# Attention of a hybrid block, written in a fixed order: two mixers' groups in turn, branch pieces in quarters

## The chip, the cores and the metric

The kernel runs on one core of one Trainium2 chip. The metric is the device time of one execution in microseconds (us), the median of a few runs. The core has five queues that work side by side: PE (TensorE, matmuls), DVE (VectorE), ACT (ScalarE), POOL (GpSimd) and SP, which issues all the DMAs here. Each takes its instructions in the order in which they stand in the program.

## The reference

One layer on x of 2048 rows and 1024 columns, all in float32. A projection feeds two attention mixers and their gates:

```python
xn = rms_norm(h, norm_gain[layer])
qa, ka, va, ga, qb, kb, vb, gb, iq, ik, iw, za, zb = jnp.split(xn @ w_in[layer], offsets, axis=-1)
ya = chunked_relpos_attention(qa, ka, va, rel_bias[layer]) * jax.nn.silu(ga)   # 8 heads, own chunk of 64 and 8 before
yb = dsa_sparse_attention(qb, kb, vb, iq, ik, iw) * jax.nn.silu(gb)            # 8 heads on one K and V, 256 keys a query
merged = sigmoid(za + b_merge[0]) * (ya @ w_branch_a) + sigmoid(zb + b_merge[1]) * (yb @ w_branch_b)
out = rms_norm(h + merged @ w_out, final_norm_gain)
```

In mixer B an indexer picks the 256 keys of each query; the kernel turns that choice into an additive mask and computes B as a dense attention over all keys up to the query's chunk.

## The kernel before

**Stages.** The first half projects x, searches the 256 keys and writes q, k, v, gates and masks to DRAM. From about 980 us on attention runs, overlapping the end of the projection; then the merged product with w_out and the last norm.

**Numbers in two halves.** A float32 operand is split into a high part (rounded by an ACT copy) and a low part (value less high part), and products take hi and lo matmuls.

**Units.** Mixer A has 32 units: a group G of 512 rows by one of 8 heads. Mixer B has 64: a block b of 128 rows by u, a pair of heads; its work grows with b, over b + 1 tiles of 128 keys. A unit's first half, one(), makes scores: for a segment of up to 512 keys two matmuls into one of two PSUM banks `s`, then one DVE instruction (L942) that adds bias or mask, writes P to SBUF and keeps the running extreme mx; when a row block is complete ACT takes the exp of it in place (L1021 for A, L1129 for B). The second half, two(), goes in packs of up to four 128x128 tiles: transposes of P into one of three PSUM banks `pt` (L1051, L1143), split() into `pth` (ACT) and `ptl`, then products with V into one of two banks `O` (L1061, L1151). A unit then closes: the halves of O are added (ACT, DVE), scaled by the sums and the gate, and split into the tiles ya or yb of its group.

**split().** With EVERY = 3 two packs of three have ACT write `pth` (L965) and DVE subtract (L966); the third has ACT write `pth` (L958) and a second copy `pf` (L959), and POOL subtract (L963), since POOL is given SBUF operands alone.

**Branch pieces.** When a group of 512 rows is complete in a mixer, branch(m, G, c) multiplies it with one of 8 column tiles of w_branch: loads dst and sig, ACT and POOL split the weight (L1189, L1190), 12 matmuls into bank `d` (helper mm3, L238), a DVE product with the gate (L1196) and a store, or, for the second mixer to reach a group, a load of the first's result, a POOL sum (L1203) and a store. There are 64 pieces; the 8 of mixer B's last group run in the tail.

**Order.** attention() takes the units in a list `seq`, A's group 0 first, then A and B mixed so that both keep pace by a cost table. It steps one() of the next unit and two() of this one in turn. Pieces come 2 (A) or 4 (B) after one unit, from a unit or two past their group. A scheduler that simulates the engines then reorders the instructions of each queue. DMAs of a unit stand two units ahead on SP.

Of the kernel before, what the change touches and what calls it, by code (L numbers as in the profile page):

```python
# [8 lines left out]
F32 = mybir.dt.float32  # L9
# [16 lines left out]
H = 8  # L26
# [7 lines left out]
EVERY, MODE = 3, 1  # L34
# [29 lines left out]
WARM = 22  # L64
WIDE = 0.8
# [32 lines left out]
def block_kernel(ctx: ExitStack, tc: tile.TileContext, io, dbg=None):  # L98
# [834 lines left out]
    def next_o(shape):  # L933
        i = rot("O", 2 if late else 1)
        return (pe, pl_ps)[i].tile(shape, F32, name="O", tag=f"O{i}")

# [8 lines left out]

    def split(hi, lo, src, n):
        turn[0] += 1
        if MODE == 3:
            c = n * SPL // 128
            nc.scalar.activation(hi, src, AF.Copy)  # L950
            pf = wk.tile([128, 512], F32, name="pf", tag="pf", bufs=PFB)[:, :n - c]
            nc.scalar.activation(pf, src[:, c:], AF.Copy)
            nc.vector.tensor_tensor(lo[:, :c], src[:, :c], f32(hi[:, :c]), op=OP.subtract)
            nc.gpsimd.tensor_tensor(lo[:, c:], pf, f32(hi[:, c:]), op=OP.subtract)
        elif EVERY and turn[0] % EVERY == 0:
            pf = wk.tile([128, 512], F32, name="pf", tag="pf", bufs=PFB)[:, :n]
            if MODE == 1:
                nc.scalar.activation(hi, src, AF.Copy)  # L958
                nc.scalar.activation(pf, src, AF.Copy)  # L959
            else:  # L960
                nc.scalar.activation(pf, src, AF.Copy)
                nc.gpsimd.tensor_copy(hi, pf)
            nc.gpsimd.tensor_tensor(lo, pf, f32(hi), op=OP.subtract)  # L963
        else:
            nc.scalar.activation(hi, src, AF.Copy)  # L965
            nc.vector.tensor_tensor(lo, src, f32(hi), op=OP.subtract)  # L966
# [3 lines left out]
    def load_a(G, h):  # L970
# [8 lines left out]
        v = ld.tile([128, 8, 128], F32R, name="vs", tag="vs")  # L979
        for i, g in enumerate(range(max(0, G - 1), G + 1)):  # L980
            nc.sync.dma_start(f32(kk[:, i * 512:i * 512 + 512]), kA[g].rearrange("l r h n -> (l r) h n")[:, h, :])
            nc.sync.dma_start(f32(v[:, 4 * i:4 * i + 4]), vA[g][h])
# [3 lines left out]
        return base, q, kk, v, bias  # L986

    def a_unit(G, h):
        st = {}

        def loads():
            st["ld"] = load_a(G, h)
            if h % 2 == 0:
                sg = ld.tile([128, 512], F32, name="sg", tag="sg", bufs=SGB)
                nc.sync.dma_start(sg, gAD[G][(h // 2) * 128:(h // 2) * 128 + 128])
                shared["sg", "a", h // 2] = sg

        def one():
            base, q, kk, v, bias = st["ld"]
            P = next_p()  # L1000
            P = P[:, :2560].rearrange("p (j n) -> p j n", j=4)
            st["P"] = P
            mx = shared["mx"] = sml.tile([128, 4], F32, name="mx", tag="mx", bufs=4)
            if h % 2 == 0:
                shared["sum", "a", h // 2] = sml.tile([128, 2, 4], F32, name="sum", tag="sum", bufs=4)
            sm = shared["sum", "a", h // 2]
            for j in range(4):
                i = 4 * G + j
                f = max(0, i - 4)
                nk = (i - f + 1) * 128  # L1010
                segs = [(0, 256), (256, 384)] if nk == 640 else [(0, nk)]
                for a, w in segs:
                    s_ps = next_s()
                    ko = (f - base) * 128 + a
                    for m in range(2):
                        nc.tensor.matmul(s_ps[:, :w], q[:, m, j * 128:(j + 1) * 128], kk[:, ko:ko + w],
                                         start=(m == 0), stop=(m == 1))
                    softmax_piece(s_ps[:, :w], bias[:, 640 - nk + a:640 - nk + a + w], a == 0,
                                  P[:, j, a:a + w], mx[:, j:j + 1])
                    yield  # L1020
                nc.scalar.activation(P[:, j, :nk], P[:, j, :nk], AF.Exp, bias=mx[:, j:j + 1], scale=-1.0,  # L1021
                                     accum_out=sm[:, h % 2, j:j + 1])

        def two():
            base, q, kk, v, bias = st["ld"]
            P = st["P"]
            O = next_o([128, 512])
# [5 lines left out]
            packs = []  # L1033
            while tiles:
                p_, room = [tiles.pop(0)], 4
                room -= p_[0][2]
                for z in list(tiles):
                    if z[2] <= room:
                        p_.append(z)
                        tiles.remove(z)  # L1040
                        room -= z[2]
                packs.append(p_)
            done = 0
            total = sum(len(p_) for p_ in packs)
            for p_ in packs:
                pt = next_pt([128, 512])
                off = 0
                for kt, j0, nj in p_:
                    for j in range(j0, j0 + nj):
                        f = max(0, 4 * G + j - 4)  # L1050
                        nc.tensor.transpose(pt[:, off:off + 128], P[:, j, (kt - f) * 128:(kt - f + 1) * 128], ident)  # L1051
                        off += 128
                ph_ = wk.tile([128, 512], F32R, name="pth", tag="pth", bufs=HB)
                pl_ = wk.tile([128, 512], F32R, name="ptl", tag="ptl", bufs=HB)
                split(ph_[:, :off], pl_[:, :off], pt[:, :off], off)
                yield
                off = 0
                for kt, j0, nj in p_:
                    w = nj * 128
                    for n_, src in enumerate((ph_, pl_)):  # L1060
                        nc.tensor.matmul(O[:, j0 * 128:j0 * 128 + w], v[:, kt - base, :], src[:, off:off + w],  # L1061
                                         start=(done == 0 and n_ == 0), stop=(done == total - 1 and n_ == 1),
                                         skip_group_check=True)
                    done += 1
                    off += w
            ty = wy.tile([128, 512], F32, name="ty", tag="ty", bufs=TYB)
            if h % 2 == 0:
                shared["y"] = wy.tile([128, 512], F32, name="y", tag="y")
            y = shared["y"]
            a0, a1 = (slice(0, 64), slice(64, 128)) if h % 2 == 0 else (slice(64, 128), slice(0, 64))  # L1070
            nc.scalar.activation(ty[a0], O[a1], AF.Copy)
            nc.vector.tensor_tensor(y[a0], O[a0], ty[a0], op=OP.add)
            yield
            if h % 2 == 1:
                yield from finish("a", G, h // 2, y, shared.pop(("sum", "a", h // 2)), shared.pop(("sg", "a", h // 2)),
                                  slice(0, 512))

        return loads, one, two

    shared = {}  # L1080

    def finish(m, G, pair, y, sm, sg, cols):

        n = 4
        nc.vector.reciprocal(sm, sm)
        rb = wz.tile([128, n, 2, HD], F32, name="rb", tag="rb", bufs=1)
        nc.gpsimd.tensor_copy(rb, sm.rearrange("p a j -> p j a")[:, :, :, None].to_broadcast([128, n, 2, HD]))
        rp = next_pt([128, 512])
        for j in range(n):
            nc.tensor.transpose(rp[:, j * 128:(j + 1) * 128], rb[:, j].rearrange("p a d -> p (a d)"), ident)  # L1090
        nc.vector.tensor_tensor(sg, rp, sg, op=OP.mult)
        nc.gpsimd.tensor_tensor(y, y, sg, op=OP.mult)
        yield
        yh, yl = y_of(m, G)
        nc.scalar.activation(yh[:, pair, cols], y, AF.Copy)
        nc.gpsimd.tensor_tensor(yl[:, pair, cols], y, f32(yh[:, pair, cols]), op=OP.subtract)

    def b_unit(b, u):

        n = 128 * (b + 1)  # L1100
        st = {}

        def loads():
            if u == 0:
                q = ldb.tile([128, H, 128], F32R, name="qsB", tag="qsB")
                nc.sync.dma_start(f32(q), qB[b // 4][b % 4].rearrange("l r h n -> (l r) h n"))
                sg = ldb.tile([128, 4, 128], F32, name="sgB", tag="sgB")
                nc.sync.dma_start(sg, gBD[b // 4].rearrange("(c p) n -> p c n", p=128)[:, :, (b % 4) * 128:(b % 4 + 1) * 128])
                if b < 2:
                    mk = mk01[:, b, :]  # L1110
                else:
                    mk = ldb.tile([128, S], BF16, name="mk", tag="mk")
                    nc.sync.dma_start(mk[:, :n], mskD[b, :, :n])
                shared["b", b] = (q, sg, mk)
# [17 lines left out]
        def two():  # L1132
            P = st["P"]
            if u % 2 == 0:
                shared["OB"] = next_o([128, 4, 128])
# [642 lines left out]
```

## Time and profile before

| | us |
|---|---|
| median of 3 runs | 2018.23 |
| the runs | 2017.92 to 2023.54 |
| profiled execution | 2020.23 |
| its span, first to last instruction | 2018.3 |

| engine | busy us | share of the span |
|---|---|---|
| PE | 1968.9 | 98% |
| DVE | 1442.0 | 71% |
| ACT | 1267.2 | 63% |
| POOL | 810.7 | 40% |

Matmuls are pipelined and their ends are modelled, so a PE that is busy 98% of the time is not one at its peak pace: waits of a tenth of a microsecond between two matmuls do not show as idle time. The distance between the starts of matmuls tells more. PEld is TensorE's weight load, which overlaps the matmuls. In the rows, "x" and a number is a count; names are out<-in.

### The profile page before, as it was taken

To read this page: it belongs to the slowest core of one execution; us is meant where nothing else is said; L and a number is where in the kernel's file an instruction comes from. 1 tells how busy PE (TensorE), PEld (TensorE's weight loads), DVE (VectorE), ACT (ScalarE), POOL (GpSimd) and SP (SyncE) were. 2 spreads that over 40 slices of the span, in tenths; PEclk is the share of its full clock that TensorE was granted. 3 is DMA by queue.
4 is the path that set the end of the run, shared out by engine and by line. 5 is a ranking of instruction groups with operands and counts; after the bars stand their busy time and mean duration, and the time that the engine had idled before them with its cause. 6 is when DMAs were issued, how large, how long until landed. Compare 5 with 4: busy or idle time off the path is not lost. (4 is left out here: it accounts for less than half of the span.)

```text
span 2018.3 us, 34087 instructions
## 1 busy us (share of the span) xinstructions
PE 1968.9 (98%) x10699; PEld 1689.3 (84%) x10699; DVE 1442.0 (71%) x3584; ACT 1267.2 (63%) x2540; POOL 810.7 (40%) x1057
## 2 busy tenths in 40 slices
PE   9999999999999999899989999999999999999998
PEld 8788888899898888678768888888988898887886
DVE  6638788797988988565556778658875688765444
ACT  6446666565476655354587879759986698773221
POOL 2222233322262454553345564464445444442420
PEclk9999999999999999999999999999999999999999
DMA  9673444555465665388998564573356531335732
GB/s 340 216 237 122 133 140 153 178 169 166 157 205 170 220 208 188 111 261 273 305 277 272 173 203 144 178 233 120 119 159 203 175 102 53 111 89 183 227 134 94
DMA packets 244731, 363.16 MB, mean 180 GB/s; under 512 B 31169, under 2 KB 115777, under 8 KB 244417
## 3 DMA queue, kind: packets, MB, share of 16 engines
q1 hardware_dynamic: 244544, 360.94, 55.8%
q8 instruction: 85, 1.39, 0.3%
q14 instruction: 102, 0.83, 0.1%
HBM read 244.23 MB, written 116.62 MB: 179 GB/s over the span
## 5 line engine op out<-in xcount | busy, mean ns | idle before, releaser
L238 PE MATMUL acc<-xh,wt 128*128 128x512 f32 x2128 | 675.5, 391 | 5.1 <-DVE wt L1393 1.6
L238 PEld LDWEIGHTS acc<-xh,wt 128*128 128x128 f32 x2128 | 398.5, 188 | 90.1 <-DVE wt L1393 2.7
L238 PE MATMUL acc<-xl,wt 128*128 128x512 f32 x1064 | 415.0, 390 | 0.1
L963 POOL TENSOR_TENSOR ptl<-pf,pth 128x512 fp32r<-128x512 f32 (+1 forms) x144 | 179.7, 1248 | 221.1 <-ACT pf L959 176.1
L238 PEld LDWEIGHTS acc<-xl,wt 128*128 128x128 f32 x1064 | 199.9, 188 | 40.8 <-DVE xl L1386 0.4
L966 DVE TENSOR_TENSOR ptl<-pt,pth 128x512 fp32r<-128x512 f32 (+1 forms) x288 | 187.0, 659 | 44.9 <-ACT pth L965 44.0
L617 DVE SCALAR_TENSOR_TENSOR sc<-lg,iw,sc 128x512 f32<-128x512 f32 (+2 forms) x266 | 178.1, 678 | 44.1 <-ACT lg L612 39.1
L1126 PE MATMUL s<-kBt,qsB 128*128 128x512 f32 (+3 forms) x640 | 188.9, 386 | 6.4 <-DMA kBt<-kB 3.2
L229 POOL TENSOR_TENSOR wt<-wst,wt 128x512 fp32r<-128x512 f32 (+1 forms) x96 | 115.9, 1236 | 182.1 <-ACT wt L228 165.6
L612 ACT ACTIVATE lg<-lg 128x512 f32<-128x512 f32 (+2 forms) x304 | 150.4, 524 | 49.5 <-PE lg L610 48.4
L965 ACT ACTIVATE pth<-pt 128x512 fp32r<-128x512 f32 (+1 forms) x288 | 159.6, 578 | 29.4 <-PE pt L1143 16.1
L1129 ACT ACTIVATE P<-P,mx 128x128 f32<-128x128 f32 (+15 forms) x128 | 154.6, 1209 | 23.0 <-DVE mx L942 22.1
L1143 PE MATMUL pt<-ident,P 128*128 128x128 f32 x1088 | 166.9, 274 | 1.8 <-DVE ptl L966 1.0
L1151 PE MATMUL O<-pth,vBt 128*128 128x256 f32 x544 | 148.4, 291 | 3.2 <-DVE yb L1161 1.1
L1151 PE MATMUL O<-ptl,vBt 128*128 128x256 f32 x544 | 148.0, 298 | 2.7 <-POOL ptl L963 1.3
L942 DVE CUSTOM_DVE_ANT_0 P<-s,mk,mx 128x512 f32<-128x512 f32 (+2 forms) x192 | 125.2, 652 | 28.7 <-PE s L1126 20.9
L1143 PEld LDWEIGHTS pt<-ident,P 128*128 128x128 f32 x1088 | 126.9, 140 | 10.8 <-DVE ptl L966 2.3
L1190 POOL TENSOR_TENSOR dw<-dst,dw 128x512 fp32r<-128x512 f32 x64 | 82.5, 1290 | 109.0 <-ACT dw L1189 108.2
L1126 PEld LDWEIGHTS s<-kBt,qsB 128*128 128x128 f32 x640 | 103.5, 192 | 19.6 <-DVE mx L942 10.0
L665 ACT ACTIVATE jk<-sc,st 128x640 int8<-128x640 f32 (+6 forms) x49 | 71.2, 1453 | 75.1 <-DVE st L683 63.5
L1151 PEld LDWEIGHTS O<-ptl,vBt 128*128 128x128 f32 x544 | 103.0, 189 | 12.8 <-DVE ptl L966 6.4
L1151 PEld LDWEIGHTS O<-pth,vBt 128*128 128x128 f32 x544 | 103.2, 190 | 11.0 <-ACT pth L965 3.4
(323 smaller groups left out, 4459.3 us busy)
## 6 DMA issues: line engine op xcount, KB each, us to landing
wst<-wP SPq DMA_DIRECT2D x80, 256.0 KB
wst<-wS SPq DMA_DIRECT2D x72, 256.0 KB
kk<-kA SPq DMA_DIRECT2D x56, 256.0 KB
vs<-vA SPq DMA_DIRECT2D x56, 256.0 KB
wst<-wS SPq DMA_DIRECT2D x72, 192.0 KB
qz<-qA SPq DMA_DIRECT2D x96, 128.0 KB
qD<-q SPq DMA_DIRECT2D x39, 256.0 KB
part<-qD SPq DMA_DIRECT2D x39, 256.0 KB
```

Source lines behind the costliest of these rows:

```text
L229: nc.gpsimd.tensor_tensor(wt[:, 1, k:k + n, c * 128:(c + 1) * 128], st, f32(hi), op=OP.subtract)
L238: m = nc.tensor.matmul(acc, a, b, start=(first and i == 0), stop=(last and i == n - 1), **({} if first and last else {"skip_group_check": ...
L612: nc.scalar.activation(lg, lg, AF.Relu)
L617: nc.vector.scalar_tensor_tensor(o_, lg, wv, o_, op0=OP.mult, op1=OP.add)
L942: nc.vector.tensor_tensor_reduce(dst, ps_, add, 1.0, FMAX if first else mx, OP.add, OP.min, accum_out=mx)
L963: nc.gpsimd.tensor_tensor(lo, pf, f32(hi), op=OP.subtract)
L965: nc.scalar.activation(hi, src, AF.Copy)
L966: nc.vector.tensor_tensor(lo, src, f32(hi), op=OP.subtract)
L1126: nc.tensor.matmul(s_ps[:, :w], q[:, h, :], kBt[:, m, a:a + w], start=(m == 0), stop=(m == 1))
L1129: nc.scalar.activation(P[:, e, :n], P[:, e, :n], AF.Exp, bias=mx[:, e:e + 1], scale=-1.0, accum_out=st["sum"][:, (u % 2) * 2 + e:(u % 2) * ...
L1143: nc.tensor.transpose(pt[:, k, e, :], P[:, e, (kt + k) * 128:(kt + k + 1) * 128], ident)
L1151: nc.tensor.matmul(o_, vBt[:, kt + k, :], src[:, k, :], start=(kt + k == 0 and n_ == 0), stop=(kt + k == b and n_ == 1), skip_group_check= ...
```

## The change

- EVERY goes from 3 to 6: one pack in six is split on POOL, not one in three.
- attention() now ends before unit 6 has been multiplied with V; the rest runs in written(), in which the order of all five queues is the order of the code, with no scheduler.
- `seq` takes whole groups in turn: A's 0, B's blocks 0 to 3 (one A unit among them), the rest of A's 1, B's 4 to 7, A's 2, B's 8 to 11, A's 3, B's 12 to 15.
- A unit is cut into score(n), turned(n) and closing(). written() counts events; an event is one segment of scores or one pack of transposes. Scores run ahead by 1.3 to 2.2 units. later(d, f) puts a step d events on: an exp 2, the low half 0, the product with V 6 or when three wait.
- A piece is an object: its loads, then 8 events on the weight's high half, then four parts of three matmuls. fill() hands out parts so that the pieces of a group end before the other mixer's next group is through.
- V, B's q with the mask, and the gates have loads of their own, at the place where their buffer comes free. The six one-column POOL copies ahead of the kBt and vBt loads are gone. Five weights of w_out and the first m tile come in steps during the last units and pieces.

The count of matmuls and of DMAs is the same. DVE has 72 subtractions more, ACT 72 copies and POOL 72 subtractions fewer.

```diff
-EVERY, MODE = 3, 1
+EVERY, MODE = 6, 1
...
-    seq = [("a", 0, h) for h in range(H)]
-    ua = [("a", g, h) for g in range(1, NG) for h in range(H)]
-    ub = [("b", b, u) for b in range(4 * NG) for u in range(4)]
...
+    seq = [("a", 0, h) for h in range(H)]
+    for i in range(4 * 4):
+        seq.append(("b", i // 4, i % 4))
+        if i in (6,):
+            seq.append(("a", 1, (6,).index(i)))
+    for g in range(1, NG):
+        seq += [("a", g, h) for h in range(H) if ("a", g, h) not in seq]
+        seq += [("b", b, u) for b in range(4 * g, 4 * g + 4) for u in range(4)]
...
+        while t_[0] < len(units):
...
+            if si < len(units) and si <= ti + 2 and ps - pt_ < 1 + min(LEADB if isinstance(units[si], BUnit) else LEADA, LEADE / events[si]):
+                exp = units[si].score(s_[1])
...
+                run_due()
+                if exp:
+                    later(EXPD, exp)
+            else:
+                if t_[1] == 0:
+                    unit_starts(ti)
+                while len(products) >= BEHIND:
+                    made[0] += 1
+                    multiply()
...
+                low, times_v = units[ti].turned(t_[1])
...
+                run_due()
+                later(LOWD, low)
+                later(OD, lambda n=n: due_product(n))
+            fill(min(t_[0], len(units) - 1), t_[1] / len(units[t_[0]].packs) if t_[0] < len(units) else 1)
+            background()
...
-    for _ in att_gen:
-        pass
-
-    load_m(0)
+    E_ = mybir.EngineType
+    with tc.manual_schedule(engines={E_.PE, E_.DVE, E_.Activation, E_.Pool, E_.SP}):
+        written()
```

The order on PE among large B units, before (s are scores, pt transposes of P, O products with V, hi from pth and lo from ptl):

```order
L1143 MATMUL pt<-ident,P 128x128 x4
L1126 MATMUL s<-kBt,qsB 128x512 x2
L1151 MATMUL O<-pth,vBt 128x256
L1126 MATMUL s<-kBt,qsB 128x512 x2
L1151 MATMUL O<-ptl,vBt 128x256
L1151 MATMUL O<-pth,vBt 128x256
L1151 MATMUL O<-ptl,vBt 128x256
L1143 MATMUL pt<-ident,P 128x128 x2
```

The same engine in mixer B after the change, with a quarter of a piece (d, from a group ya of mixer A and its weight dw):

```order
L1188 MATMUL pt<-ident,P 128x128 x4
L1175 MATMUL s<-kBt,qsB 128x512 x2
L1175 MATMUL s<-kBt,qsB 128x256 x2
L1201 MATMUL O<-pth,vBt 128x256
L1201 MATMUL O<-ptl,vBt 128x256
L1188 MATMUL pt<-ident,P 128x128 x4
L254 MATMUL d<-ya_16847,dw 128x512
L254 MATMUL d<-ya_16848,dw 128x512
L254 MATMUL d<-ya_16847,dw 128x512
L1175 MATMUL s<-kBt,qsB 128x512 x2
```

Before, the scheduler set scores between a high product and its low one; now a pack's products stand together, after the next packs' transposes. A piece before stands on PE like this, between scores of mixer A and transposes of mixer B:

```order
L1016 MATMUL s<-kk,qz 128x256 x2
L1143 MATMUL pt<-ident,P 128x128 x2
L238 MATMUL d<-yb_14570,dw 128x512
L238 MATMUL d<-yb_14571,dw 128x512
L238 MATMUL d<-yb_14570,dw 128x512 x2
L238 MATMUL d<-yb_14571,dw 128x512
L238 MATMUL d<-yb_14570,dw 128x512 x2
```

All twelve matmuls follow each other there; after the change no more than three do (the fence before). On ACT among large B units before, with the exp (P), the high halves and the second copies:

```order
L1129 ACTIVATE P,sumB<-P,mx 128x1792
L958 ACTIVATE pth<-pt 128x512
L959 ACTIVATE pf<-pt 128x512
L965 ACTIVATE pth<-pt 128x512 x2
L1129 ACTIVATE P,sumB<-P,mx 128x1792
L958 ACTIVATE pth<-pt 128x512
```

And on ACT after, with a piece's weight (dw):

```order
L1179 ACTIVATE P,sumB<-P,mx 128x1792
L993 ACTIVATE pth<-pt 128x512 x3
L1272 ACTIVATE dw<-dst 128x512
L1179 ACTIVATE P,sumB<-P,mx 128x1792
L993 ACTIVATE pth<-pt 128x512
L990 ACTIVATE pth<-pt 128x256
```

The exp keeps its place among the packs, three to four of them from one to the next; half of the second copies are gone.

More of the change, by code (lines that the diff above doesn't have):

```diff
@@ L64 @@
 WARM = 22
+AT8 = 5
+MSTEP = 2
+LASTA = 3
+ADD = 2
+READY = 5
+GAP = 4
+OD = 6
+PREP = 8
+MARGIN = 4
+LEADA = 0.3
+LEADB = 1.2
+LEADE = 5
+EXPD = 2
+LOWD = 0
+BEHIND = 3
+GATES = 6
 WIDE = 0.8
@@ L944, in block_kernel @@
     turn = [PH]
[L946 to L966, printed above, removed]
     qz = []
@@ L1010, in one @@
                 nk = (i - f + 1) * 128
[L1011 to L1027, printed above, removed]
+                for a, w in [(0, 256), (256, 384)] if nk == 640 else [(0, nk)]:
+                    self.segs.append((j, (f - base) * 128 + a, a, w, nk))
             tiles = []
@@ L1041, in two @@
                         room -= z[2]
[L1042 to L1046, printed above, removed]
-                off = 0
[L1048 to L1058, printed above, removed]
+                self.packs.append(p_)
@@ new lines, in turned, with times_v @@
+        def turned(self, n):
+            pt = next_pt([128, 512])
+            off = 0
+            for kt, j0, nj in self.packs[n]:
+                for j in range(j0, j0 + nj):
+                    f = max(0, 4 * self.G + j - 4)
+                    nc.tensor.transpose(pt[:, off:off + 128], self.P[:, j, (kt - f) * 128:(kt - f + 1) * 128], ident)
+                    off += 128
+            ph_ = wk.tile([128, 512], F32R, name="pth", tag="pth", bufs=HB)
+            pl_ = wk.tile([128, 512], F32R, name="ptl", tag="ptl", bufs=HB)
+            low = splitter(ph_[:, :off], pl_[:, :off], pt[:, :off], off)
+            def times_v():
+                if n == 0:
+                    self.O = bank_of([128, 512])
+                off = 0
+                for kt, j0, nj in self.packs[n]:
@@ L1063, in two @@
                                          skip_group_check=True)
-                    done += 1
+                    self.done += 1
                     off += w
[L1066 to L1096, printed above, removed]
@@ new lines, in branch @@
+    def branch(m, G, c):
+        p_ = Piece(m, G, c)
+        p_.fetch()
+        p_.high()
+        p_.low()
+        for k in range(4):
+            p_.part(k)
+        p_.out()
+        p_.join()
+        p_.store()
+    kv_at = {}
+    seq = [("a", 0, h) for h in range(H)]
+    for i in range(4 * 4):
[5 more added lines that the diff above has]
+        seq += [("b", b, u) for b in range(4 * g, 4 * g + 4) for u in range(4)]
@@ L1236, in block_kernel @@
+    at = {z: i for i, z in enumerate(seq)}
+    units = [AUnit(g, i) if m == "a" else BUnit(g, i) for m, g, i in seq]
+    for g in range(1, NG):
+        kv_at[at["b", 4 * g, 0] - KVO] = g
     ws = {}
@@ new lines, in early, with fetch @@
+        ws[k] = hi, lo
+        steps = []
+        for hf in range(2):
+            c_ = slice(hf * 512, hf * 512 + 512)
+            st = []
+            def fetch(st=st, c_=c_):
+                st.append(ld.tile([128, 512], F32, name="ost", tag="bias"))
+                nc.sync.dma_start(st[0], io["wO"][:, k, c_])
+            steps += [fetch, lambda st=st, c_=c_: nc.scalar.activation(hi[:, c_], st[0], AF.Copy),
+                      lambda st=st, c_=c_: nc.vector.tensor_tensor(lo[:, c_], st[0], f32(hi[:, c_]), op=OP.subtract)]
@@ L1282, in load_kv, with scores_of, rest_of @@
         nc.sync.dma_start(f32(vBt[:, 4 * g:4 * g + 4, :]), vB[:, 4 * g:4 * g + 4, :])
+    def scores_of(un):
+        for n in range(len(un.segs)):
+            exp = un.score(n)
+            yield
+            if exp:
+                exp()
+    def rest_of(un):
+        for n in range(len(un.packs)):
+            low, times_v = un.turned(n)
+            low()
+            yield
+            times_v()
+        before_, after_ = un.closing()
+        for f_ in after_[:2]:
+            f_()
+        yield
+        if before_:
+            for f_ in before_ + after_[2:3]:
+                f_()
+            yield
+            for f_ in after_[3:]:
+                f_()
     def attention():
[L1285 to L1287 removed]
+        units[0].loads()
+        units[1].loads()
+        for _ in scores_of(units[0]):
             yield
[L1289 to L1298 removed]
+        for i in range(H - 2):
+            units[i + 2].loads()
+            live = [scores_of(units[i + 1]), rest_of(units[i])]
             while live:
```

601 lines of the change are left out of this document (425 added, 176 removed).

## The prediction

> **What bounds the kernel now.** I read the page's first lines, then the busy time by stage, then the groups of matmuls inside the attention stage, then starts in the timeline, and last who waited for whom.
>
> ```profile
> span 2018.3 us, 34087 instructions
> ```
>
> The profiled execution took 2020.2 us, 1.9 around this span; the median of the three timed runs is 2018.2, so 2.0 come off a sum made against the profiled time.
>
> ```profile
> core 0: us, PE busy (x) PEld busy (x) DVE busy (x) ACT busy (x) POOL busy (x), PEclk, DMA share, GB/s
> 975.00:1046.00 71.00, 61.16 (x316) 50.61 (x314) 43.06 (x119) 55.47 (x127) 26.31 (x33) 0.95 0.97 299
> 1046.00:1830.00 784.00, 765.22 (x4946) 676.02 (x4947) 572.61 (x1554) 610.79 (x1209) 376.18 (x361) 1.00 0.50 158
> ```
>
> The changed code runs from about 1046 to 1830: 784 us, where TensorE shows 765 busy. That figure hides waits, since matmuls overlap and their ends are modelled. So I count what TensorE has to do there and price it by starts.
>
> ```profile
> L1143 PE MATMUL pt<-ident,P 128*128 128x128 f32 x1088 | 166.9, 274 | 1.8 <-DVE ptl L966 1.0 <-ACT P L1129 0.3 <-ACT pf L959 0.2
> L1126 PE MATMUL s<-kBt,qsB 128*128 128x512 f32 x400 | 131.7, 416 | 3.1 <-DVE mx L942 3.0
> L1051 PE MATMUL pt<-ident,P 128*128 128x128 f32 x490 | 75.1, 275 | 0.9 <-DVE ptl L966 0.8
> L1126 PE MATMUL s<-kBt,qsB 128*128 128x384 f32 x112 | 31.1, 364 | 0.2 <-DVE mx L942 0.2
> L1126 PE MATMUL s<-kBt,qsB 128*128 128x256 f32 x112 | 25.4, 310 | 0.0
> L1168 PE MATMUL pt<-ident,rbb 128*128 128x128 f32 x64 | 12.3, 274 | 1.8 <-DVE sg L1091 0.8 <-DVE sgB L1171 0.8
> L1090 PE MATMUL pt<-ident,rb 128*128 128x128 f32 x52 | 7.9, 275 | 0.0
> ```
>
> The other lines have one width each, or equal shares of several, so one row of each line over the stage does (first PE busy with its count): the B products L1151, 256 wide; the A products L1061, a quarter each 512, 384, 256 and 128 wide; the A scores L1016, half 384 and half 256; tile d, the branch pieces, 512; tile po, matmuls of the tail that already stand here, 512.
>
> ```profile
> 1046.00:1830.00 784.00, 197.07 (x1088) 158.17 (x1088) 1.00 0.50 158
> 1046.00:1830.00 784.00, 92.81 (x400) 64.59 (x400) 1.00 0.50 158
> 1046.00:1830.00 784.00, 91.35 (x384) 60.15 (x384) 1.00 0.50 158
> 1046.00:1830.00 784.00, 172.70 (x666) 120.81 (x666) 38.59 (x56) 1.00 0.50 158
> 1046.00:1830.00 784.00, 18.25 (x74) 13.59 (x75) 0.00 (x0) 1.00 0.50 158
> ```
>
> The price of one is the distance of starts where nothing waits; the first column is the start:
>
> ```profile
> 1859.94 1.52 PE L1646 MATMUL po<-wosy,mm 128*128 128x512 f32 x6
> 1861.30 0.61 PE L1646 MATMUL po<-wos,mm 128*128 128x512 f32 x2
> ```
> ```profile
> 1746.34 0.28 PE L1151 MATMUL O<-ptl,vBt 128*128 128x256 f32 x1
> 1746.46 0.28 PE L1151 MATMUL O<-pth,vBt 128*128 128x256 f32 x1
> ```
> ```profile
> 1749.21 0.60 PE L1143 MATMUL pt<-ident,P 128*128 128x128 f32 x4
> 1749.56 0.48 PE L238 MATMUL d<-ya,dw 128*128 128x512 f32 x1
> ```
>
> A 512-wide matmul takes 1.36/6 = 0.227 us, a 256-wide 0.12, four transposes 0.35 (0.0875 each, used for 128-wide products too); 384-wide lies between, 0.172. Need: 512-wide 400+100+666+74 = 1240, 281 us; 384-wide 192+112+100 = 404, 69; 256-wide 1088+192+112+100 = 1492, 179; transposes 1088+490+64+52 = 1694, 148; 100 narrow products, 9. Together 686 us of 784: TensorE loses 98 us here, 12.5%. No change of order can bring more than that.
>
> Where is it lost? Two stretches, all instructions and then tile d (the branch pieces) alone:
>
> ```profile
> 1280.00:1360.00 80.00, 79.97 (x474) 70.66 (x474) 44.51 (x114) 47.09 (x91) 48.77 (x44) 1.00 0.69 222
> 1360.00:1480.00 120.00, 117.68 (x814) 104.80 (x813) 103.86 (x297) 109.03 (x211) 47.49 (x49) 1.00 0.40 128
> ```
> ```profile
> 1280.00:1360.00 80.00, 45.64 (x183) 33.23 (x183) 10.36 (x15) 1.00 0.69 222
> 1360.00:1480.00 120.00, 2.21 (x6) 0.99 (x6) 0.00 (x0) 1.00 0.40 128
> ```
>
> Pieces stand in a heap: 183 of their matmuls in 80 us, 6 in the next 120. With them DVE is busy 56% and ACT 59%; without them 87% and 91%. The same count by shape in these stretches (21 and 20 groups, first and last shown) gives a need of 76 us in 80 and 104 in 120: 4.5% lost beside pieces, 14% without.
>
> ```profile
> L238 PE MATMUL d<-yb,dw 128*128 128x512 f32 x96 | 24.0, 398 | 0.0
> ...
> L1090 PE MATMUL pt<-ident,rb 128*128 128x128 f32 x4 | 0.6, 273 | 0.0
> ```
> ```profile
> L1126 PE MATMUL s<-kBt,qsB 128*128 128x512 f32 x91 | 29.5, 414 | 0.1
> ...
> L1090 PE MATMUL pt<-ident,rb 128*128 128x128 f32 x8 | 1.2, 272 | 0.0
> ```
>
> TensorE's weight loads wait for VectorE first of all, for a free s bank:
>
> ```profile
> PEld s L1126 <- DVE mx L942: 10.0, 25, 1.6
> ```
>
> **The change part by part.**
>
> *Splitting every sixth pack on POOL, not every third.*
>
> ```profile
> L966 DVE TENSOR_TENSOR ptl<-pt,pth 128x512 fp32r<-128x512 f32 (+1 forms) x276 | 180.4, 664 | 38.7 <-ACT pth L965 37.8
> L963 POOL TENSOR_TENSOR ptl<-pf,pth 128x512 fp32r<-128x512 f32 (+1 forms) x138 | 171.9, 1246 | 217.9 <-ACT pf L959 172.9 <-PE s L1126 14.8 <-PE pt L1143 9.0
> L959 ACT ACTIVATE pf<-pt 128x512 f32<-128x512 f32 (+1 forms) x137 | 79.5, 581 | 0.0
> ```
>
> 72 subtractions move. DVE gets 72 x 0.664 = +48 us (573 to 620), ACT loses 72 x 0.581 = 42 (611 to 569), POOL 72 x 1.25 = 90. TensorE's 686 stays the largest, DVE next with 90% of it. Cover: the added DVE work lies beside matmuls as long as DVE keeps up, and nothing else covers it; below I price that cover gone.
>
> *Groups in turn, pieces spread, scores ahead, products up to three packs behind.* No matmul is added or removed. All 56 pieces of the stage (the 56 DVE products in the row of tile d) are cut into quarters of three matmuls and laid over the next group of the other mixer; with each move two loads, an ACT copy, a POOL subtraction, a DVE product and a store, for second halves also a load and a POOL sum. So every stretch gets the mean mix: with a stage of T us DVE has 620/T and ACT 569/T. Ends for T: if all of it loses what the stretch with pieces loses, 686/0.955 = 718, and there DVE would need 620/718 = 86%, just what it reached in the stretch without pieces (87%); so 718 is the good end by two rows. The bad end: DVE keeps the 573/784 = 73% that it has over the stage, 620/0.73 = 849. I take a 7% loss, T = 738, nearer the good end: it asks 84% of DVE, which rows show it can give over 120 us, and the loss of 14% was seen at ACT 91%, which now has 77%. Gain 784 - 738 = 46, between +66 and -65.
>
> Does taking the mixers in turn undo the even mix? DVE's softmax pieces:
>
> ```profile
> L942 DVE CUSTOM_DVE_ANT_0 P<-s,mk,mx 128x512 f32<-128x512 f32 x104 | 77.7, 747 | 18.7 <-PE s L1126 14.6
> L942 DVE CUSTOM_DVE_ANT_0 P<-s,bias,mx 128x384 f32<-128x384 f32 x92 | 56.5, 614 | 16.6 <-PE s L1016 14.2
> L942 DVE CUSTOM_DVE_ANT_0 P<-s,bias 128x256 f32<-128x256 f32 x92 | 38.5, 418 | 7.8 <-PE s L1016 5.3 <-issue 1.4 <-PE pt L1051 0.6
> ```
>
> An A unit gives DVE 4 x (0.614 + 0.418) + 5 x 5/6 x 0.664 = 6.9 us, and one piece and its closing add some 1.4: 8.3. It gives TensorE 8 x (0.172 + 0.12) + 20 x 0.0875 + 4 x (0.227 + 0.172 + 0.12 + 0.0875) = 6.5, and 12 x 0.227 = 2.7 for its piece: 9.2. DVE 90%. A B unit of 14 key tiles: DVE 7 x 0.747 + 7 x 5/6 x 0.664 + 1.0 = 10.1; TensorE 14 x 0.227 + 28 x (0.0875 + 0.12) + 1.4 = 10.4; DVE 97%. Both are near the mean of 90%, and neither passes TensorE, so turns cost nothing by these rows.
>
> The Trainium skill (Perfetto Trace Analysis, "Optimization Strategy") advises to interleave regimes whose most-contended engine differs. That speaks for the spread pieces, where the two stretches agree, and against mixers in turn, where the unit sums do not bear it out. If turns cost what the heaps cost, the gain would be 0 and not 46.
>
> *Loads.* The number of DMAs is unchanged. V now has its own loads, issued behind the last product of the unit that frees the buffer, so that no other load stands behind that wait. TensorE's rows above name no load but one kBt at the start, so this is worth 0; the same loads hide under a unit of 6 to 12 us. Behind a late store of a piece (it waits for the sum on POOL) the next dst, sig and q loads would be late: I take 0, ends -3 and +5, as they are issued eight steps ahead.
>
> *The six small POOL copies ahead of the kBt and vBt loads* go: 0, they gate only SP.
>
> *Start of the stage.* The stretch 975 to 1046 keeps its order by the scheduler (71 us, 61 busy, clock 0.95): 0, ends -3 and +3. At the handover the kBt load must still land: 0. If the first B units (one to four key tiles, short chains) find no A unit to cover them, a few us are lost; within the 7%.
>
> *End.* Three of the five output weights and the first m tile are loaded in steps during the last units, not after them: -2, ends -5 and +2.
>
> Sum: 2020.2 - 46 - 2 = 1972 for the profiled execution, 1970 for the median; I say 1972, the 2 us being below anything the terms can tell.
>
> **The rivals.**
>
> *DVE becomes the bound (slower).* DVE has 620 us to do in order. Each low half waits for its high half on ACT, and there the copy stands behind an exp:
>
> ```profile
> L1129 ACT ACTIVATE P<-P,mx 128x128 f32<-128x128 f32 (+15 forms) x128 | 154.6, 1209 | 23.0 <-DVE mx L942 22.1 <-DVE sumB L1163 0.4
> ```
>
> 128 of these at 1.21 us mean; in a fixed order the softmax behind a waiting low half waits too, then the s banks, then TensorE. It decides at a DVE use of 620/784 = 79%: below it the kernel is slower. At 75%, between that and the 73% of the whole stage, T = 827, and the time is 2061. For it: DVE's idle before low halves, 37.7 us by ACT. Against it: 87% was reached without pieces, and products stand two rounds, some 2.6 us, behind their transposes.
> The Trainium skill (Perfetto Trace Analysis, "Optimizing Scalar/DVE Operations") says to offload a saturated DVE, even to GpSimd, which the change undoes; by it, were DVE the bound, its 48 us would all come back, and 46 of gain would become none.
>
> *Turns cost what the pieces gain (same).* A large B unit has DVE at 97% of TensorE's need and no A unit beside it to lend slack. If that brings back the 14% lost in the stretch without pieces, T is 686/0.86 = 798 at most, and some 784 if a quarter of the stage loses 7%: 2018, the gain of spread pieces spent on turns. Against it: the A units beside them before were no lighter for DVE, 6.9 us against 6.5 of TensorE even at one in six.
>
> *Less than half (faster).* 10% lost, T = 762: 1995.
>
> *More (faster).* 3 to 4% lost, T = 711: 1943. It asks DVE for 87% over the whole stage.
>
> **How the numbers follow.** Forecast (T from 725 to 755) 0.50; more 0.18; less than half 0.10; same 0.08; slower 0.14. So faster by over 0.3% (6 us, about what a measurement here can tell from no change) 0.78, within 0.08, slower 0.14. The range 1940 to 2020 leaves out about 0.05 below, and the slower case above.
>
> **What would show it.** Right: stage from 1046 near 740 us, tile d in every 40 us of it, DVE near 84% and ACT near 77% throughout, POOL's low halves halved, no stretch with ACT over 90%. Wrong: weight loads waiting longer for mx of DVE than the 10.0 above, DVE below 79% with idle before low halves, or waits for kk, vs, dst on TensorE and ACT.

## The result and the profile after

The changed kernel takes 2005.4 us (median of 2003.0, 2004.5, 2006.2 and 4586), the kernel before 2019.2 beside it: ratio 0.9928, 95% interval 0.9913 to 0.9943. The execution of 4586 us was disturbed and is left out of the ratio. So the change gains 14 us, 0.7%; the forecast was 46.

The page's first lines, and the busy time by stage (columns PE, PEld, DVE, ACT, POOL, then the granted clock, the DMA share and GB/s):

```profile
span 2004.4 us, 33826 instructions
PE 1956.1 (98%) x10699; PEld 1690.6 (84%) x10699; DVE 1485.3 (74%) x3656; ACT 1242.3 (62%) x2468; POOL 722.1 (36%) x979
```
```profile
975.00:1046.00 71.00, 58.91 (x313) 48.66 (x312) 46.55 (x124) 52.67 (x121) 20.15 (x26) 0.98 0.96 302
1046.00:1100.00 54.00, 47.56 (x285) 41.65 (x284) 36.07 (x120) 41.17 (x114) 20.65 (x26) 0.94 0.64 196
1100.00:1820.00 720.00, 708.34 (x4683) 639.69 (x4683) 571.89 (x1506) 548.50 (x1035) 271.26 (x264) 1.00 0.50 158
1400.00:1500.00 100.00, 100.00 (x693) 92.27 (x692) 84.63 (x217) 81.35 (x143) 32.60 (x35) 1.00 0.25 78
```

DVE carries 79% of the long stretch and ACT 76%, and among the large units 85% and 81%, near the 84% and 77% that the prediction asked for. As amounts of work, DVE has 608 us from 1046 to 1820 (620 computed) and ACT 590 (569 computed): of the 42 us that ACT was to lose it lost 21. What became of the other 21 is not known. Tile d now stands everywhere (three of the stretches of 40 us):

```profile
1120.00:1160.00 40.00, 15.73 (x57) 10.05 (x57) 2.74 (x4) 1.00 0.90 273
1440.00:1480.00 40.00, 8.12 (x27) 4.70 (x27) 1.37 (x2) 1.00 0.23 71
1760.00:1800.00 40.00, 2.57 (x9) 1.60 (x9) 0.69 (x1) 1.00 0.31 93
```

So the pieces are spread as planned, and the stage still ends only 14 us sooner: the last product with V starts at 1808.2 us, before at 1822.5. The reason is in the starts of the matmuls. First the kernel before, the place from which the prediction took its price for transposes, with what follows it; then the changed kernel (first column start, second duration):

```profile
1749.21 0.60 PE L1143 MATMUL pt<-ident,P 128*128 128x128 f32 x4
1749.56 1.87 PE L238 MATMUL d<-ya,dw 128*128 128x512 f32 x7
1751.27 0.28 PE L1151 MATMUL O<-pth,vBt 128*128 128x256 f32 x1
```
```profile
1442.34 0.60 PE L1188 MATMUL pt<-ident,P 128*128 128x128 f32 x4
1442.69 0.94 PE L254 MATMUL d<-ya,dw 128*128 128x512 f32 x3
1443.47 0.62 PE L1175 MATMUL s<-kBt,qsB 128*128 128x512 f32 x2
1443.93 0.28 PE L1201 MATMUL O<-pth,vBt 128*128 128x256 f32 x1
```

The four transposes seem to take 0.35 us, as the prediction has it. But the three 512-wide matmuls behind them take 0.78 and not 3 x 0.23 = 0.69 (before, seven take 1.71 and not 1.61); the two scores after those take 0.46, their price. In 186 distances inside such groups of the changed kernel (1400 to 1500 us) the median is 0.109 us; the matmul after a group starts 0.028 us after the last transpose, and the one after that comes 0.08 late. A group of four therefore costs 4 x 0.109 = 0.44 us, not 0.35.

With 0.109 for a transpose, 0.2295, 0.174 and 0.119 for 512, 384 and 256 columns and 0.085 and 0.06 for narrower ones, I subtract from the distance of each two starts the price of the first, and add up what is left ("lost") over all matmuls. From 960 us to the end TensorE loses 73.2 us before and 59.4 after: the difference, 13.8, is the whole gain (the spans differ by 13.9), as it must be where both kernels have the same matmuls. The loss holds waits, and also what a lower granted clock adds: in the changed kernel the clock is 0.5 three times for 3.4 us between 990 and 1062 us, 5 us of the 59, and then not again until its last matmul; before, four times up to 1069 us, 6 of the 73. By place:

| | before: need, lost | after: need, lost |
|---|---|---|
| 960 to 1046 us | 68.6, 18.3 | 67.7, 18.2 |
| 1046 to 1100 | 43.8, 9.1 | 41.1, 12.9 |
| 1100 to the last product with V | 676.5, 46.5 | 680.1, 28.4 |
| of it: heaped pieces, 1280 to 1360 | 79.2, 0.8 | |
| of it: no pieces, 1360 to 1480 | 110.5, 9.5 | |
| of it: 1400 to 1520 | | 119.0, 0.9 |
| of it: change of groups, 1520 to 1600 | | 72.7, 7.3 |

### The profile page after: what moved, and what is told of

Read it like the earlier page. It is cut to its first block, busy times and chain, and to the rows that moved or that the text cites. A ratio compares the mean times of both kernels' runs of the same rounds, so it can differ in the third digit from the quotient of the medians.

```text
span 2004.4 us, 33826 instructions
## 1 busy us (share of the span) xinstructions
PE 1956.1 (98%) x10699; PEld 1690.6 (84%) x10699; DVE 1485.3 (74%) x3656; ACT 1242.3 (62%) x2468; POOL 722.1 (36%) x979
## 5 line engine op out<-in xcount | busy, mean ns | idle before, releaser
L993 ACT ACTIVATE pth<-pt 128x512 fp32r<-128x512 f32 (+1 forms) x360 | 205.7, 576 | 115.2 <-PE pt L1188 76.2
L994 DVE TENSOR_TENSOR ptl<-pt,pth 128x512 fp32r<-128x512 f32 (+1 forms) x360 | 238.3, 662 | 36.9 <-ACT pth L993 35.7
L633 DVE SCALAR_TENSOR_TENSOR sc<-lg,iw,sc 128x512 f32<-128x512 f32 (+2 forms) x266 | 178.2, 678 | 43.8 <-ACT lg L628 38.8
L1175 PE MATMUL s<-kBt,qsB 128*128 128x512 f32 (+3 forms) x640 | 195.1, 392 | 6.8 <-DVE mx L954 4.4
L992 POOL TENSOR_TENSOR ptl<-pf,pth 128x512 fp32r<-128x512 f32 (+1 forms) x72 | 89.4, 1242 | 198.4 <-ACT pf L991 103.0
L1201 PE MATMUL O<-ptl,vBt 128*128 128x256 f32 x544 | 142.9, 283 | 0.9 <-POOL ptl L992 0.6
L1062 PE MATMUL s<-kk,qz 128*128 128x256 f32 (+1 forms) x448 | 109.5, 333 | 7.0 <-DVE mx L954 6.9
L254 PE MATMUL d<-yb,dw 128*128 128x512 f32 x384 | 109.5, 404 | 3.4 <-POOL dw L1275 2.1
```

The costliest lines, as they stand in the source:

```text
L254: m = nc.tensor.matmul(acc, a, b, start=(first and i == 0), stop=(last and i == n - 1), **({} if first and last else {"skip_group_check": ...
L633: nc.vector.scalar_tensor_tensor(o_, lg, wv, o_, op0=OP.mult, op1=OP.add)
L994: return lambda: nc.vector.tensor_tensor(lo, src, f32(hi), op=OP.subtract)
L1175: nc.tensor.matmul(s_ps[:, :w], q[:, 2 * u + e, :], kBt[:, m, a:a + w], start=(m == 0), stop=(m == 1))
L1201: nc.tensor.matmul(o_, vBt[:, kt + k, :], src[:, k, :], start=(kt + k == 0 and n_ == 0), stop=(kt + k == b and n_ == 1), skip_group_check= ...
```

## The experiments

All are the changed kernel with one edit, but for e9; the ratio is against the kernel before on the same chip, and the loss is the sum just described, split into the first 100 us of TensorE's work from 960 us on (the start) and the next 700 (the stage).

| kernel | median us | ratio, 95% interval | lost: start, stage, whole |
|---|---|---|---|
| before | 2017 to 2019 | 1 | 27.2, 48.0, 73.2 |
| changed | 2005.4 | 0.9928, 0.9913 to 0.9943 | 30.7, 30.2, 59.4 |
| e1 split every third pack | 2016.9 | 1.0003, 0.9991 to 1.0015 | 32.4, 38.9, 69.5 |
| e2 pieces heaped | 2058.1 | 1.0208, 1.0185 to 1.0231 | 29.6, 79.0, 108.1 |
| e3 mixed list | 2100.0 | 1.0405, 1.0385 to 1.0425 | 31.7, 118.4, 153.6 |
| e4 scheduler | 2031.3 | 1.0076, 1.0054 to 1.0098 | 31.3, 52.8, 83.2 |
| e6 no pack on POOL | 2005.1 | 0.9935, 0.9921 to 0.9949 | 29.6, 31.3, 61.4 |
| e7 weights 12 events ahead | 2017.7 | 1.0001, 0.9993 to 1.001 | 32.7, 38.5, 69.2 |
| e8 q first | 2007.6 | 0.9952, 0.9939 to 0.9964 | 29.6, 30.5, 60.3 |
| e9 before, every sixth pack | 2022.9 | 1.0018, 1.0008 to 1.0027 | 25.2, 50.4, 74.8 |
| e10 weights 6 events ahead | 2017.2 | 0.9998, 0.9986 to 1.001 | 28.7, 43.6, 71.0 |
| e11 more A units early | 2031.3 | 1.0073, 1.006 to 1.0086 | 33.2, 51.5, 83.8 |

The experiments ran in three sets, each beside the kernel before, and the changed kernel was not timed again. Differences from it in the text are between medians; by the ratios every experiment comes out 1 to 4 us slower still (e1 15 us, not 12; e12 gains 33, not 34). e5 and e12 change TensorE's work and are told below. In every row the loss differs from that of the kernel before as the profiled spans do, within 2.5 us. The whole has the tail as well (-2 to +3.5 us).

Three theories name why only 14 us came. The *price theory*: TensorE needs some 40 us more than the prediction counted, since transposes cost 0.109 us, so most of the 98 us "lost" was work. The *DVE theory*: the 48 us that DVE took over make it the bound. The *turns theory*: what spread pieces gain is lost by taking the mixers in turn.

### e1: every third pack on POOL again

```diff
-EVERY, MODE = 6, 1
+EVERY, MODE = 3, 1
```

> The changed kernel with every third pack split on POOL again: DVE has 72 subtractions fewer (48 us), ACT 72 copies more (42 us). Price theory (TensorE already runs at its pace in most of the stage, because a group of four transposes costs 0.44 us and not 0.35): 2005, within 6 us either way. DVE theory (DVE's 48 us more hold TensorE up, so the forecast gain was lost there): 1965 to 1990.

Measured: 2016.9 us, as slow as the kernel before and outside both expectations. From 1100 to 1820 us, DVE has 35 us less and POOL 79 more:

```profile
1100.00:1820.00 720.00, 704.77 (x4657) 634.23 (x4656) 536.68 (x1436) 571.96 (x1091) 349.83 (x326) 1.00 0.49 157
```

Relief of DVE gains nothing; it costs 12 us. That refutes the DVE theory and shows that in the fixed order the split by six is worth nearly as much as the whole change. The extra loss is spread over all the stage and no single wait carries it, so which step of the longer way over POOL costs the time stays open.

### e2: pieces not spread

```diff
-            credit[0] = min(credit[0] + rate, 3.0)
+            credit[0] = 3.0
```

> The changed kernel with the pieces of a group handed out as soon as they are ready, not spread. If the even mix of pieces makes the gain: 2013 to 2020. If the order of scores, transposes and products makes it: 2005, within 6 us.

Measured: 2058.1, 53 us slower than the changed kernel and far outside both expectations. Two neighbouring stretches, the first with 96 matmuls of pieces (eight pieces), the second with none:

```profile
1400.00:1480.00 80.00, 77.97 (x503) 69.13 (x501) 57.51 (x153) 54.54 (x99) 27.50 (x27) 1.00 0.36 116
1480.00:1560.00 80.00, 77.73 (x566) 72.31 (x565) 71.62 (x190) 68.51 (x128) 20.53 (x23) 1.00 0.20 65
```

DVE has 72% in the one and 90% in the other, and TensorE loses 4.4 us of the first 80 and 5.2 of the second. So heaping makes DVE's work uneven, as before. But these 160 us hold only 9.6 of the 79 us that the stage loses. More is lost where heaps start: 12.4 us from 1309 to 1371 and 10.7 from 1530 to 1592. There ACT waits 3.7 and 3.4 us for the loads of weights, TensorE's pieces wait for ACT's and POOL's halves of them, and the granted clock falls to 0.5 for 3.4 us each time. The run shows that the fixed order needs the spread, and is worse than the scheduler without it; how much of that is uneven DVE work and how much late pieces it does not separate.

### e3: the mixed list of units

In place of whole groups in turn, `seq` is made by the cost table of the kernel before; all else stays.

```diff
-        seq += [("a", g, h) for h in range(H) if ("a", g, h) not in seq]
-        seq += [("b", b, u) for b in range(4 * g, 4 * g + 4) for u in range(4)]
+    while ua or ub:
+        if ua and (not ub or done[0] / ta < done[1] / tb):
+            z = ua.pop(0)
...
```

> The changed kernel with the unit list of the kernel before (A and B units mixed by the cost table). Turns theory (taking the mixers in turn costs what spreading gains): 1985 to 1998. Price theory: turns cost little, 2002 to 2012.

Measured: 2100.0, 95 us slower than groups in turn. No theory expected that. Tile d in two stretches, then the wait of ACT for weights from 1100 to 1820 us, here and in the changed kernel (us in total, times, longest):

```profile
1360.00:1400.00 40.00, 25.64 (x103) 18.30 (x102) 6.22 (x9) 1.00 0.64 212
1440.00:1480.00 40.00, 0.00 (x0) 0.00 (x0) 0.00 (x0) 1.00 0.27 84
```
```profile
ACT dw L1272 <- DMA dst<-wB: 48.6, 11, 9.0
```
```profile
ACT dw L1272 <- DMA dst<-wB: 10.3, 8, 2.8
```

TensorE itself waits here for DVE to empty the bank of the piece before, and DVE for the store of an earlier result (in the changed kernel 0.8 us for the first and no row for the second):

```profile
PE d L254 <- DVE dt L1285: 23.8, 13, 5.0
DVE dt L1285 <- DMA mD<-dt: 43.2, 10, 7.3
```

In a mixed list the groups of both mixers end close together, so their pieces come together and are heaped again, and their loads and stores come late. After 1100 us the granted clock is 0.5 for 31 us in all, which holds 15 of the stage's 118 us of loss. The run does not price the turns by themselves; it shows that turns and spread are one thing in this code, since one mixer's pieces need the other's group to lie on.

### e4: the scheduler instead of the fixed order

```diff
-    with tc.manual_schedule(engines={E_.PE, E_.DVE, E_.Activation, E_.Pool, E_.SP}):
-        written()
+    written()
```

> The changed kernel's code, but its order handed to the scheduler again, which may reorder all five queues. If the fixed order makes the gain: 2012 to 2022. If the list of units, the pieces and the split make it: 2005, within 6 us.

Measured: 2031.3, 26 us slower and outside both expectations. Tile d shows one thing that differs: under the scheduler the quarters stand together again, 74 matmuls in one stretch and none in the next three.

```profile
1640.00:1680.00 40.00, 19.16 (x74) 13.01 (x72) 4.82 (x7) 1.00 0.44 138
1680.00:1720.00 40.00, 0.00 (x0) 0.00 (x0) 0.00 (x0) 0.91 0.13 41
```

Another has nothing to do with pieces. The scheduler put the split of a weight of w_out (wosy) at 1675 to 1686 us into ACT's and DVE's queues (1780 to 1804 in the changed kernel), and both stood behind its load:

```profile
ACT wosy L1350 <- DMA ost<-wO: 4.4, 1, 4.4
PE O L1201 <- ACT pth L993: 3.8, 1, 3.8
```

TensorE stood 3.8 us up to 1686.5 us, and the granted clock was 0.5 from 1685.6 to 1692.4 (hence the 0.91 above). From 1674 to 1700 us it loses 9.0 us, of the 22 by which the stage's loss exceeds the changed kernel's. So e4 prices this scheduler's order, not the quarters alone.

### e5: every group of transposes twice

```diff
-            off = 0
-            for kt, j0, nj in self.packs[n]:
+            for again_ in range(2):
+              off = 0
+              for kt, j0, nj in self.packs[n]:
...
-            for k in range(nk):
+            for k in [*range(nk)] * 2:
```

The transposes of P are issued a second time into the same bank: 1648 more, nothing else. This measures the price by itself.

> The changed kernel with every group of transposes of P issued twice into the same bank (1648 transposes more on TensorE, nothing else). Price theory (0.109 us each, as the starts inside a group show): 2005 + 180 = 2185. The prediction's price (0.0875): 2149. If TensorE had slack there (waits that the added work fills), less: 2100 to 2140.

Measured: 2162.5, 157 us more (ratio 1.0724, interval 1.0708 to 1.0739), between two expectations. The starts decide:

```profile
1440.79 1.04 PE L1075 MATMUL pt<-ident,P 128*128 128x128 f32 x8
1441.58 0.48 PE L1176 MATMUL s<-kBt,qsB 128*128 128x256 f32 x2
1441.90 0.34 PE L1088 MATMUL O<-pth,vs 128*128 128x384 f32 x1
```

From the first of eight transposes to the start that follows the two matmuls behind them pass 1.11 us = 8 x 0.109 + 2 x 0.119; by 0.0875 it would be 0.94. At 0.0875 the 1648 would add 144 us, less than the 157 measured. At 0.109 they add 180 us of work, of which 24 fell into waits (loss 35.5 instead of 59.4); 180 - 24 = 156, measured 157. After 1100 us TensorE now loses only 9.2 us, 1.1%, since the other queues have 157 us more for the same work. So the price theory holds, and what the changed kernel still loses there is waiting for others' results, which more work of TensorE's covers.

### e6: no pack on POOL

```diff
-EVERY, MODE = 6, 1
+EVERY, MODE = 0, 1
```

> The changed kernel with no pack split on POOL: DVE has 72 subtractions more again (48 us), ACT 72 copies fewer. DVE theory: DVE is at its limit, 2020 to 2050. If the long way of a pack over ACT, ACT and POOL is what costs (as every third instead of every sixth cost 12 us): 1995 to 2003. Price theory alone: 2005, within 6 us.

Measured: 2005.1, as the changed kernel, with DVE at 84% of the long stretch and 90% among the large units:

```profile
1100.00:1820.00 720.00, 707.41 (x4678) 638.84 (x4677) 603.55 (x1569) 520.06 (x968) 191.66 (x198) 1.00 0.51 157
1400.00:1500.00 100.00, 100.00 (x693) 92.27 (x692) 89.97 (x229) 76.61 (x132) 18.53 (x24) 1.00 0.26 78
```

Another 72 subtractions on DVE, 48 us by their own durations (32 of busy time in the long stretch), cost nothing. DVE is not the bound here, and POOL's help is not needed.

### e7 and e10: a piece's weight split 12 or 6 events after its load, not 8

```diff
-PREP = 8
+PREP = 12
```

> The changed kernel with twelve events instead of eight between a piece's loads and its weight's high half. If late weights (5.7 us of ACT waiting for dst between 1515 and 1600, and TensorE's weight loads waiting for POOL's dw) are lost time: 1998 to 2003. If they are not: 2005, within 4 us.

In e10 the same line is `PREP = 6`.

> The changed kernel with a piece's weight split 6 steps after its load and not 8 (12 had cost 12 us). If the cost of 12 was the long time that a piece holds its buffers and its late store, shorter helps a little or is neutral: 2000 to 2006. If the weights' loads then come late for ACT's high half (it already waited 5.7 us in 1515 to 1600), 2008 to 2015.

Measured: 2017.7 and 2017.2, beyond all four expectations: either way the whole gain is gone. For 6 the trace of e10 shows a place, ACT first, then PE (in brackets the wait):

```profile
1152.28 0.63 ACT L1272 ACTIVATE dw<-dst 128x512 fp32r<-128x512 f32 x1 [5.68 <-DMA dst<-wB]
1152.94 0.60 ACT L993 ACTIVATE pth<-pt 128x512 fp32r<-128x512 f32 x1
```
```profile
1154.41 1.08 PE L1074 MATMUL pt<-ident,P 128*128 128x128 f32 x4 [3.72 <-DVE ptl L994]
1155.44 1.01 PE L1062 MATMUL s<-kk,qz 128*128 128x384 f32 x2
```

ACT waits 5.7 us for a weight; the high half behind it in its queue waits too, DVE's low half waits for that, and TensorE 3.7 us for the bank. A late load stops the queue, not only its own step. And the wait costs more than itself: the granted clock is 0.5 from 1153.4 to 1160.2 us, the four transposes above take 1.03 us to the next start and not 0.35, and a 512-wide matmul takes 0.43. From 1140 to 1170 us TensorE loses 8.9 us (0.4 in the changed kernel), most of e10's 12. Two more waits for weights, of 1.6 and 1.5 us at 1319 and 1548 us, are each followed by 3.4 us at 0.5. For 12 I found no such place: it loses 3 us more from 1060 to 1120 and 6 more from 1280 to 1380, in many small waits, with the clock full after 1064 us. Why a longer lead costs as much stays open.

### e8: the first q loads ahead of the K and V loads

```diff
+        load_q(0)
         load_kv(0)
+        load_q(1)
         for b in range(2):
-            load_q(b)
             load_gates(b)
```

> The changed kernel with mixer B's first q loaded ahead of kBt and vBt, and the gates last. If the order of the first loads costs the 2.4 us that TensorE waits for q at 1043: 2002 to 2004. If the DMA engines are simply full there (share 0.96 from 975 to 1046): 2005, within 2 us.

Measured: 2007.6, no gain. At the handover the changed kernel waits for loads of several kinds and for DVE:

```profile
1045.41 0.63 PE L1175 MATMUL s<-kBt,qsB 128*128 128x128 f32 x4 [2.40 <-DMA qsB<-qB]
1051.40 0.58 PE L1087 MATMUL O<-pth,vs 128*128 128x512 f32 x1 [2.18 <-DMA vs<-vA]
1057.82 0.38 PE L1175 MATMUL s<-kBt,qsB 128*128 128x256 f32 x1 [1.82 <-DVE mx L954]
```

In e8 the waits for qsB and vs are gone, but from 1035 to 1062 us TensorE then waits 3.1 us for DVE's mx and 2.5 for ACT, and loses 12.5 us there (13.4 in the changed kernel); the start's loss stays at 29.6. So it was not the order of the first loads. The DMA engines are at 96% from 975 to 1046 us, but that they set the pace is not shown.

### e9: the kernel before with the split by six

```diff
-EVERY, MODE = 3, 1
+EVERY, MODE = 6, 1
```

> The kernel before, with one pack in six split on POOL and nothing else changed. In the changed kernel the split by six was worth 12 us against the split by three (2016.9 against 2005.4). If that gain is POOL's slow low halves being waited for, it comes under the scheduler too: 2006 to 2012. If it hangs on the fixed order (the scheduler already stands other work where a low half is late), the time stays at 2015 to 2021, or goes up by some us since DVE is loaded more in the stretches without pieces, where it was at 87%: 2019 to 2030.

Measured: 2022.9, slightly slower. Under the scheduler and the old list the split by six gains nothing; e1's 12 us belong to the changed kernel's order. Which part of that order they need was not tested.

### e11: three A units among the first B units, not one

```diff
-        if i in (6,):
-            seq.append(("a", 1, (6,).index(i)))
+        if i in (2, 6, 10):
+            seq.append(("a", 1, (2, 6, 10).index(i)))
```

> The changed kernel with three units of mixer A's group 1 between the small units of mixer B's blocks 0 to 3, and not one. From 980 to 1100 us TensorE still loses 31 us, more than the 28 of the whole rest. If the small units of B with their short chains lack other work, two more A units fill some of it: 1999 to 2003. If the loads there set the pace (16 DMA engines at 96% from 975 to 1046), more A units bring more loads and nothing is gained: 2004 to 2012.

Measured: 2031.3, 26 us slower. Not the loads of the start, as I had expected of the worse case, but pieces that had to be issued at once (PE, in brackets the wait):

```profile
1115.17 4.04 PE L254 MATMUL d<-ya,dw 128*128 128x512 f32 x10 [0.62 <-POOL dw L1275]
1120.09 3.01 PE L254 MATMUL d<-ya,dw 128*128 128x512 f32 x12 [0.88 <-DVE dt L1285]
```

Whole pieces stand behind each other there, and the second 100 us of TensorE's work lose 24.6 us instead of 5.9.

### e12: low products of mixer B left out

```diff
-                    for n_, src in enumerate((ph_, pl_)):
+                    for n_, src in enumerate((ph_,)):
...
-                                         stop=(kt + k == b and n_ == 1), skip_group_check=True)
+                                         stop=(kt + k == b and n_ == 0), skip_group_check=True)
```

> The changed kernel with the low products of mixer B left out (the matmuls of ptl with V; the low halves are still computed): 544 matmuls of 256 columns fewer, 544 x 0.1187 = 64.6 us of TensorE's work in a stage whose other queues keep theirs. If TensorE's work is the bound with room on the others, nearly all comes back: 1941 to 1950. If DVE with 620 us (79% of the stage) is close to a bound of its own near 85%, the stage can't go below some 730 of 763 us: 1970 to 1990.

Measured: 1971.6 (ratio 0.9765, interval 0.975 to 0.9779), 34 us of the 65 came back, inside the second expectation. Among the large units:

```profile
1400.00:1500.00 100.00, 98.93 (x648) 87.45 (x646) 94.00 (x246) 89.19 (x161) 34.71 (x37) 1.00 0.28 93
```

TensorE loses 4.8% there (0.6% in the changed kernel) with DVE at 94% and ACT at 89%. So in the changed kernel TensorE's own work is the bound among the large units, and the next one lies close: half of the work saved here was lost on waits. No version tried beats the changed kernel; e6 equals it.

## Why the prediction was right and wrong

**The step that failed is the need.** The price in it, "four transposes 0.35 (0.0875 each, used for 128-wide products too)", was read from the distance between the first transpose and the next matmul's start, and that matmul starts early. With the prices above the stage from 1046 to 1830 us needs 726 us, not 686, and before it lost 56 us (7.1%), not 98 (12.5%). Of the forecast T of 738, 726 was work: it asked for a loss of 1.6%, although I meant 7%. The good end of 718 and the 711 of the rival *More* lay below the work itself.

**The second failure follows from it.** "4.5% lost beside pieces, 14% without" was 1.0% and 7.9%: the "loss" beside pieces was nearly all transposes. That spreading removes the 7.9% was right where it applies: from 1400 to 1520 us the changed kernel loses 0.8%. But I gave the mean mix to "every stretch". The first 54 us of the stage lose 12.9 us (9.1 before), and 1520 to 1600, a change of groups, 7.3 of 80. Over 1046 to 1816, the same work 14 us shorter, the changed kernel loses 42 us, 5.5%, so 14 of the 56 came back. Only a split of the stage into steady stretches and group changes could have said 14.

**Ends and direction.** The gain of 14 lies between the ends +66 and -65, and faster had 0.78. That the sign came out as forecast is in part luck: with the need of 726 the chosen loss of 7% gives T = 781 against 784, which is no change.

**The split on POOL.** That DVE's 48 us are hidden was right (e6 moves 72 more subtractions to it for nothing). But it was no free step: without it the rest gains 0 (e1), and alone it loses 4 (e9). I had no term for a gain from it. The low halves of the stage are as computed (second number in brackets: forms):

```profile
L994 DVE TENSOR_TENSOR ptl<-pt,pth 128x512 fp32r<-128x512 f32 (+1 forms) x343 | 228.3, 666 | 34.4 <-ACT pth L993 33.3 <-POOL ya L1137 0.4
L992 POOL TENSOR_TENSOR ptl<-pf,pth 128x512 fp32r<-128x512 f32 (+1 forms) x69 | 85.6, 1241 | 192.6 <-ACT pf L991 97.2 <-DVE mx L954 48.8 <-DVE ptl L994 12.3
```

**Rivals.** *DVE becomes the bound* was to decide at 79% of DVE; from 1046 to 1820 it has 608/774 = 79% and the kernel is faster, and e6 runs 84%. The threshold was no limit of DVE, only its 620 us divided by the old length of the stage; 608 of them fell here. TensorE's weight loads for scores do not wait longer for VectorE than before (B's scores, 1046 to 1820; 10.0 before):

```profile
PEld s L1175 <- DVE mx L954: 7.1, 11, 2.0
```

*Turns cost what the pieces gain* is not borne out: the stretch of B units alone, 1400 to 1520, is the best of the stage (with a transpose at 0.109 a large B unit gives DVE 92% of TensorE's need, not the 97% of the prediction); what turns cost at the group changes was not measured by itself. *Less than half* (10% lost, 1995) is where it came out nearest, for another reason than the one given there.

The Trainium skill (Perfetto Trace Analysis, "Optimization Strategy"), which advises to interleave regimes with different most-contended engines, agrees with this case for the pieces: heaping them costs 53 us (e2). For a saturated DVE it says that offloading work, even to GpSimd, may make sense, and warns that between these two it might not help ("Optimizing Scalar/DVE Operations"); the prediction left the warning out. Here DVE at 79% was not saturated (e6 runs at 84% for the same time), and more of its work on POOL was 12 us slower (e1).

**Loads** at nothing: nearly. ACT waits 10.3 us for weights in the long stretch, 5.7 of it in 1515 to 1605, where TensorE loses most:

```profile
ACT dw L1272 <- DMA dst<-wB: 5.7, 3, 2.8
```

e10 shows that a lead two events shorter costs 12 us. **Start** 0, ends -3 and +3: the loss up to 1100 us is 3.7 us larger, of it none before 1046, and whether the first B units lacked cover stays open: more A units (e11) did not help. **End** -2: from the last product with V to the last po start 187.8 us, before 187.2; no gain. The first po, though, starts 8.0 us earlier (1786.3 for 1794.4).

## What to carry to other kernels

Price an instruction over a closed run of starts, group and what follows it, and test the prices where nothing can wait: if a stretch where nothing waits still shows 4.5% lost, as here, suspect the price before the schedule. Take the loss that an order can win stretch by stretch, and leave the handovers and group changes as they are unless something in the change speaks to them. When a run loses more than its waits add up to, look at the granted clock behind them (e10). In a hand-written order lead times and the split of work between queues are part of the order: here shifting one of them by a few events, or one pack in six, was worth nearly the whole change.

## What the runs showed of the hardware

- A float32 transpose of 128x128 takes 0.109 us on TensorE, in groups of two, four or eight; the matmul behind the group starts 0.028 us after the last one, and the next is then 0.08 us late (0.314 from score to score of 512 columns, not 0.231).
- PE "busy" is no measure here: 98% of the long stretch in the changed kernel (708 of 720 us), where the starts say 4% lost, and 97% in e2 in a stretch that loses 6% (77.73 of 80 us, 5.2 lost).
- With DVE at 90% busy over 100 us and TensorE's need at 99% 0.5 us of 100 is lost (e6, 1400 to 1500); at 94%, with ACT at 89%, 4.8% (e12).
- A wait of TensorE can be followed by a lower granted clock: in e10 behind waits of 3.7, 1.6 and 1.5 us it is 0.5 for 6.8, 3.4 and 3.4 us, and in the first of these a 512-wide matmul takes 0.43 us instead of 0.23. Not every wait is: the one of 2.4 us before 1045.41 in the changed kernel is followed by none until 1051.6.
